# Seven products for gate pairs, the output projection and FFN-out, with the residual kept in DRAM and tables fetched by ACT's queue

## The chip, the cores and the metric

The kernel runs on one core of a Trainium2 chip. The metric is the time of one execution in device microseconds; the median of three runs stands for a kernel. A profile is one further execution with the hardware profiler on, and its times, which are used for all durations here, are in microseconds unless marked ns. TensorE appears as PE (matmuls) and PEld (weight loads), VectorE as DVE, ScalarE as ACT, GpSimd as POOL, SyncE as SP; SPq is SP's queue, from which DMAs are issued.

## The reference

Two layers act on 256 tokens of width 2048, all in float32. A layer is

```python
h = rms_norm(x, g_mix_pre)
proj = h @ w_in                      # 2048 x 11776
u_pool, u_conv, q, k, v, g_ret, gate_pre = split(proj)
y_pool = pool_mixer(u_pool) @ w_pool_proj      # trailing means, 512 -> 2048
y_conv = conv_module(u_conv) @ w_conv_proj     # GLU, causal conv of 31 taps, layer norm, swish
y_ret = retention(q, k, v, g_ret) @ w_ret_proj # 8 heads, rotary, decay, group norm, gate
merged = sigmoid(gate_0) * y_pool + sigmoid(gate_1) * y_conv + sigmoid(gate_2) * y_ret
x = x + rms_norm(merged @ w_out, g_mix_post)
h = rms_norm(x, g_ffn_pre)
a, b = split(h @ w_ffn_in)           # 2048 x 11264
x = x + rms_norm((silu(a) * b) @ w_ffn_out, g_ffn_post)   # 5632 x 2048
```

Nearly all the arithmetic is in the products with `w_in`, `w_ffn_in`, `w_ffn_out` and `w_out`.

## The kernel before

**Products.** The tokens are two halves h of 128. A weight matrix is worked off in chunks of 512 columns; a chunk has kt k-tiles of 128 rows (16 for a width of 2048). One product is one k-tile of one chunk for one half. To keep float32's precision in the faster `fp32r` type, each operand is split into a rounded part and a rest (hi and lo), and a product is three matmuls of 128x128 by 128x512 into one PSUM bank: hi by hi, lo by hi, hi by lo (L747, L748, L749). Activations are split once, by `split` (L127), after a transposition (`transpose4`, L137): four k-tiles of a half in one slot. Weights are split as they come: `load` (L699) takes a block of two k-tiles, fetched by SP's queue into one of six `raw` buffers, casts it on ACT (L725) and subtracts on DVE (L726). There are seven such blocks (`WBLOCKS`), and `load_ahead` keeps them filled.

**Seven products.** Where a chunk n and its partner n + 1 take the same activations, four k-tiles of both, for both halves, form a 2x2 by 2x2 block product, here called a quad: 16 products (2 k-tiles x 2 x 2 x 2 blocks). Seven block products (Winograd's form of Strassen's scheme) do with 14. The kinds are b11, t1, b21, b22, t2, t3 and t4. `load` makes the differences of raw weights they need on DVE (L705, L712, L729, L730), `token_sums` (L174) the sums of activations, and `mixed_product` (L752) puts the results together from PSUM: b11 is copied to a `dt` tile by ACT (L770), t2, t3 and t4 are added to it on DVE (L785 to L797). The banks of b11, t1, t2 and t3 are of the tag `sc`, of which there are four; transpositions and the small matmuls of the jobs use the same four. Plain products accumulate in two `mm` banks for each half. Before the change, only FFN-in's pairs (silu part and linear part) have such a quad, the last one (k-tiles 12 to 15), and the first pair of each layer has none: it is `paired`, its two chunks interleaved plainly.

**Order.** `chunks` (L607 to L640) lists the chunks of a layer: pool stream, v, q, k, swish gate (two each), the conv stream's gate and value, then gates and branch projections, the output, and FFN in four parts of 3, 3, 3 and 2 pairs, each followed by the share of FFN-out that its hidden columns feed, added up in the `og` slots. `items` is the list of k-tiles in order. The main loop (L898) issues half 0's product, and when half 0 is more than `LAG` = 8 items ahead, half 1's; mixed items do both halves at once. Each product counts a tick, and `defer` runs a function so many ticks later (the transposing of results is deferred by 7 or 14).

**Jobs.** Pooling, the convolution, retention and the rotary tables are generators in the list `jobs`. After a product of half 1 of the plain kind, `run_jobs` adds `BUDGET` = 0.35 to a credit (at most 1) and steps the jobs in list order while the credit is above zero; each step yields its cost. A step that yields `WAIT` rests its job for 8 ticks. At most two jobs that aren't `light` are stepped; the convolution is light, with 124 steps of 0.35. Chunks have `needs`: at their first k-tile, `finish` (L325) steps jobs, those not light or named, two at a time in list order, until none named is left, without rests. The code's order is a priority; a scheduler fixes each engine's order from it when the program is built.

**Around it.** `post_collect`, `post_norm` and `pre_norm_quad` (L202 to L240, L161) norm the result of a sub-layer, add it to the residual `xs`, held in SBUF throughout, and make the next activations `xT`. Twenty general buffers of 4 KB a partition (`slot`) hold activations and results; `dt` (two buffers) holds decay and band tables and the sums of the seven products. All DMAs are issued by SP. The beginning (`begin`, L823) is ordered by hand on all engines but GpSimd.

Of the kernel before, what the change touches and what calls it, by code (L numbers as in the profile page):

```python
# [18 lines left out]
P = 128  # L19
# [20 lines left out]
SLOTS = 20  # L40
# [10 lines left out]
N_WARM = 12  # L51

# [23 lines left out]
def trunk(ctx: ExitStack, tc: tile.TileContext, x, x_cols, positions, g_mix_post, g_ffn_post, w_in, pool_w,  # L76
# [38 lines left out]
    xs = []  # L115
    for h in range(2):
        xs.append(cpool.tile([P, 4, NB], F32, name=f"x{h}"))
# [25 lines left out]
    def square_sum(src, acc):  # L143
        j = t2("junk", 1)
        act.activation(j, src, ACT.Square, accum_out=acc)
# [14 lines left out]

    def pre_norm_quad(h, c, gain, mixed):  # L161
        tp, g = transpose4(xs[h][:, c, :]), gain[:, 4 * c:4 * c + 4]
        if not (mixed and c == 3):
            st["xT", h].append(split(tp, g))
            return
        if h == 0:
            st["u"] = slot([P, 2, 4, P])
        u = st["u"][:, h]
        dve.tensor_tensor(u, tp, g.unsqueeze(2).to_broadcast([P, 4, P]), op=ALU.mult)
        st["xT", h].append(split(u))  # L170
        if h == 1:
            defer(6, token_sums)

    def token_sums():  # L174

        u = st["u"]
# [3 lines left out]
        dve.tensor_tensor(s[:, 1], s[:, 0], a11, op=ALU.subtract)  # L180
        dve.tensor_tensor(s[:, 2], a11, a21, op=ALU.subtract)
        dve.tensor_tensor(s[:, 3], a12, s[:, 1], op=ALU.subtract)
        hi, lo = slot([P, 4, 2, P], F32R), slot([P, 4, 2, P], F32R)
        act.copy(hi, s)
        dve.tensor_tensor(lo, s, hi.bitcast(F32), op=ALU.subtract)
        st["S"] = (hi, lo)
# [6 lines left out]
    def sum_squares(h):  # L193
        ssq = small("ssq_n", 4)
        for c in range(4):
            square_sum(xs[h][:, c, :], ssq[:, c:c + 1])
        pre_norm_rstd(h, ssq)

    def load_x(h, c):
        nc.sync.dma_start(xs[h][:, c, :], x[0, h * P:(h + 1) * P, c * NB:(c + 1) * NB])  # L200
# [19 lines left out]
    def post_norm(h, gain, mixed=False):  # L220
# [3 lines left out]
        def residual(c):  # L224
            xc = xs[h][:, c, :]
# [14 lines left out]
        defer(N_FIRST + N_STEP * 4, sum_squares, h)  # L240

# [127 lines left out]
    def pool_job(l, h):  # L369
        if h == 0:  # L370
            pw = slot([P, 4, P])
            nc.sync.dma_start(pw, pool_w[l].rearrange("g c d -> c g d"))
            st["pw"] = pw
        u, pw = st["upool"], st["pw"]
        tabs = []
        for n in ((0,) if h == 0 else (1, 2)):
            b = t2("dt", 2, (P, 4, P))
            nc.sync.dma_start(b, bands[n])
# [16 lines left out]
    def ret_job(l, h, qd):  # L395
# [4 lines left out]
        if h == 0:  # L400
            dt = t2("dt", 2, (P, 4, P))
            nc.sync.dma_start(dt, decays[qd])
# [9 lines left out]
        else:  # L412
            for pr in range(2):
                dt = t2("dt", 2, (P, 4, P))
                nc.sync.dma_start(dt, decays[2 + qd * 2 + pr])
# [97 lines left out]
    def ev_swish(l, qd):  # L513
        def f(h, ps):
# [5 lines left out]
            add_job(("ret", h), ret_job(l, h, qd))  # L520
        return f

    def ev_gate(h, ps):
        s = t2("sg", 3)
        act.activation(s, ps, ACT.Sigmoid, scale=st["rstd", h])  # L525
        st["sg", h] = s

    def ev_y(b, c):
        def f(h, ps):
            if b == 0:  # L530
                if c % 2 == 0:
                    st["mt", h, c // 2] = slot([P, 2, NB])
                dve.tensor_tensor(st["mt", h, c // 2][:, c % 2, :], ps, st["sg", h], op=ALU.mult)
# [3 lines left out]
            dve.tensor_tensor(t, ps, st["sg", h], op=ALU.mult)  # L537
            gp.tensor_tensor(m, m, t, op=ALU.add)  # L538
            if b == 1:
                if c == 0:  # L540
                    st["mT", h] = []
                defer(2 * D_T, lambda: st["mT", h].append(split(transpose4(m))))
        return f

    def gain_tile(c, h, src):
        if h == 0:
            g = t2("gp", 2)
            nc.sync.dma_start(g, src[c * NB:(c + 1) * NB].partition_broadcast(P))
# [9 lines left out]
    def ev_out(l, c):  # L558
        def f(h, ps):
            bc = gain_tile(c, h, g_mix_post[l])  # L560
            og_tile(c, h)
            post_collect(h, c, ps, bc)
            if c == 3:
                post_norm(h, par[l][:, C_GFFN:C_GFFN + 16], True)
        return f

    def ev_a(h, ps):
        t = t2("sg", 3)
        act.activation(t, ps, ACT.Silu, scale=st["rstd", h])  # L569
        st["sg", h] = t  # L570

    def ev_b(first):
        def f(h, ps, mixed=False):
            if first:
                st["hid", h] = []
            t = t2("ta", 3)
            if mixed:
                dve.tensor_tensor(t, st["sum", h], ps, op=ALU.add)  # L578
                ps = t
            dve.scalar_tensor_tensor(t, ps, st["rstd", h], st["sg", h], op0=ALU.mult, op1=ALU.mult)  # L580
            hid = st["hid", h]
            defer(D_T, lambda: hid.append(split(transpose4(t))))
        return f

    def ev_a_sum(h, t, y):

        u = t2("ta", 3)
        dve.tensor_tensor(u, t, y, op=ALU.add)  # L588
        ev_a(h, u)

    def ev_ffn(l, c, part, last):
        def f(h, ps):
            if part == 0:
                act.copy(og_tile(c, h), ps)
                return
            o = st["og", h, c]
            dve.tensor_tensor(o, o, ps, op=ALU.add)  # L597
# [3 lines left out]
            post_collect(h, c, o, bc)  # L601
            if c == 3:
                post_norm(h, par[l + 1][:, C_GPRE:C_GPRE + 16] if l + 1 < DEPTH else None)
# [5 lines left out]

    def add(w, r0, kt, c0, lhs, evac, needs=()):  # L610
        chunks.append((w, r0, kt, c0, lhs, evac, needs))

    for l in range(DEPTH):
        wi = w_in[l]
        add(wi, 0, 16, Q_POOL, "xT", ev_pool(l))
# [8 lines left out]
        add(wi, 0, 16, Q_CG, "xT", ev_conv_g)  # L624
        add(wi, 0, 16, Q_CA, "xT", ev_conv_a(l))
        for b, c in [(b, c) for c in range(4) for b in (0, 2)] + [(1, c) for c in range(4)]:
            add(wi, 0, 16, Q_GATE + b * D + c * NB, "xT", ev_gate)
            w, name = ((w_pool_proj, "pool"), (w_conv_proj, "conv"), (w_ret_proj, "ret"))[b]
            add(w[l], 0, 8 if b == 2 else 4, c * NB, ("brT", b), ev_y(b, c), (name,))
        for c in range(4):  # L630
            add(w_out[l], 0, 16, c * NB, "mT", ev_out(l, c))
        ends.append(len(chunks))
        parts = ((0, 3), (3, 6), (6, 9), (9, 11))
        for p, (b0, b1) in enumerate(parts):
            for j in range(b0, b1):
                add(w_ffn_in[l], 0, 16, j * NB, "xT", ev_a)
                add(w_ffn_in[l], 0, 16, HIDDEN + j * NB, "xT", ev_b(j == b0))
            for c in range(4):
                add(w_ffn_out[l], b0 * 4, (b1 - b0) * 4, c * NB, "hid", ev_ffn(l, c, p, p == len(parts) - 1))
        ends.append(len(chunks))  # L640

    paired = {0} | {e for e in ends[:-1]}
    fast = {n for n, ch in enumerate(chunks) if ch[5] is ev_a and n not in paired}
    items = []
    count = {}

# [4 lines left out]
    while n < len(chunks):  # L653
        if n in fast:
            for k in (0, 2, 4, 6, 8):
                plan("", n, k)
            plan("b11", n, 12)
            plan("t1", n, 12)
            plan("", n, 10)
            plan("b21", n, 14)  # L660
            plan("b22", n, 14)
            plan("", n + 1, 0)
            plan("t2", n, 12)
            plan("", n + 1, 2)
            plan("t3", n, 12)
            plan("", n + 1, 4)
            plan("t4", n, 14)
            for k in (6, 8, 10):
                plan("", n + 1, k)
            n += 2  # L670
        else:
            side = (n, n + 1) if n in paired else (n,)
            for k in range(0, chunks[n][2], LOAD):
                for m in side:
                    plan("", m, k)
            n += len(side)
# [75 lines left out]
    def mixed_product(kind, n, k, w):  # L752

        kk, last = k % 2, k % 2 == 1

        def x_part(h):
            a = st["xT", h][k // 4]
# [204 lines left out]
```

## Time and profile before

| | before |
|---|---|
| median of 3 runs (lowest, highest) | 2876.71 us (2876.64, 2877.05) |
| the profiled execution | 2875.82 us |
| its span | 2874.1 us |
| PE, DVE, ACT busy | 2855.9, 1947.7, 1356.4 us |
| products (three matmuls each) | 4056 |
| granted TensorE clock | 0.999 |
| DMA | 555.07 MB, mean 193 GB/s |

A group's line in the profile names the source line, engine, operation, what it writes and reads (out<-in) and how often, then the busy time and the mean of one in ns, then how long its engine sat idle before it and who ended that. A row of waits names who waited for whom: total us, times, longest us. A row of the windows is the stretch, its length, then busy us of PE, PEld, DVE, ACT and POOL (instructions in brackets), the granted clock, the share of the DMA engines and GB/s. A row of the chain in order of time is start, length, engine, tile and line. PE's busy time counts overlapping matmuls, so the spacing of matmuls, not their length, tells their cost.

### The profile page before, as it was taken

What the parts mean: (1) busy time and instruction counts of PE and PEld (TensorE: products, weight loads), DVE (VectorE), ACT (ScalarE), POOL (GpSimd) and SP (SyncE); (2) the same over time, 40 slices, a digit from 0 to 9 for tenths busy, and PEclk for the clock granted to TensorE, in tenths of its full rate; (3) what the DMA queues carried; (4) which work ended last, traced back from release to release, by engine and by line L of the source; (5) the groups of instructions that cost most, each with busy time, mean ns of one, the idle gap of its engine ahead of it and who ended that gap; (6) DMA issues with size and microseconds to landing.
All of it is one profiled execution on the core that took longest, in us unless ns stands there. A gap on an engine that the chain in (4) does not pass through costs nothing.

```text
span 2874.1 us, 34293 instructions
## 1 busy us (share of the span) xinstructions
PE 2855.9 (99%) x12932; PEld 2362.9 (82%) x12932; DVE 1947.7 (68%) x2253; ACT 1356.4 (47%) x1547; POOL 83.1 (3%) x102
## 2 busy tenths in 40 slices
PE   9999999999999999999999999999999999999998
PEld 7788888888888888888888888888888888888887
DVE  6766965555775776857765569555567757668586
ACT  5444445444644544544554444444455454445353
POOL 0000000000000000000000000001000000000000
PEclk9999999999999999999999999999999999999999
DMA  8655565556565656555655555655565555666554
GB/s 298 193 183 176 186 199 189 191 189 203 174 204 174 215 196 201 176 203 175 229 188 185 189 171 188 199 189 186 191 204 190 190 185 189 211 194 200 187 183 153
DMA packets 289862, 555.07 MB, mean 193 GB/s; under 512 B 17824, under 2 KB 21152, under 8 KB 289696
## 3 DMA queue, kind: packets, MB, share of 16 engines
q1 hardware_dynamic: 289696, 552.89, 58.5%
q8 instruction: 101, 1.65, 0.2%
q14 instruction: 65, 0.53, 0.1%
HBM read 550.72 MB, written 2.10 MB: 192 GB/s over the span
## 4 chain that ended last, share of the span: by engine, by line
PE 98%; DVE 1%; DMA 0%; POOL 0%; ACT 0%; issue 0%; SPq 0%; DVEq 0%; POOLq 0%; ACTq 0%
PE mm L748 32%; PE mm L749 32%; PE mm L747 32%; PE tp L140 2%; DVE x L226 0%; PE sc L429 0%; PE tp L421 0%; PE sc L385 0%; DVE wlo L726 0%; DVE ta L131 0%; DMA dt<-in_bands 0%; DMA par<-in_params 0%; POOL rpost_a L210 0%; PE sc L411 0%; PE tp L406 0%
## 5 line engine op out<-in xcount | busy, mean ns | idle before, releaser
L726 DVE TENSOR_TENSOR wlo<-raw,whi 128x1024 fp32r<-128x1024 f32 (+1 forms) x1085 | 1336.9, 1240 | 738.0 <-ACT whi L725 725.6
L725 ACT CAST whi<-raw 128x1024 fp32r<-128x1024 f32 (+1 forms) x1085 | 1135.4, 1052 | 1283.5 <-PE mm L748 1148.2
L747 PE MATMUL mm<-whi,slot 128*128 128x512 f32 x4056 | 1589.9, 392 | 1.9 <-ACT whi L725 1.7
L748 PE MATMUL mm<-whi,slot 128*128 128x512 f32 x4056 | 1581.1, 390 | 0.2
L749 PE MATMUL mm<-wlo,slot 128*128 128x512 f32 x4056 | 1580.9, 390 | 0.0
L749 PEld LDWEIGHTS mm<-wlo,slot 128*128 128x128 f32 x4056 | 761.8, 188 | 159.4 <-DVE wlo L726 0.7
L747 PEld LDWEIGHTS mm<-whi,slot 128*128 128x128 f32 x4056 | 762.0, 188 | 156.7 <-ACT whi L725 2.4
L748 PEld LDWEIGHTS mm<-whi,slot 128*128 128x128 f32 x4056 | 762.4, 188 | 156.1 <-DVE slot L134 2.1
L342 DVE SCALAR_TENSOR_TENSOR slot<-slot,par,slot 128x229 f32<-128x229 f32 (+23 forms) x240 | 101.9, 479 | 0.3
L134 DVE TENSOR_TENSOR slot<-tp,slot 128x512 fp32r<-128x512 f32 x60 | 41.2, 687 | 50.3 <-ACT slot L133 50.3
L133 ACT CAST slot<-tp 128x512 fp32r<-128x512 f32 x60 | 35.2, 586 | 83.3 <-PE tp L140 83.3
L538 POOL TENSOR_TENSOR slot<-slot,tb 128x512 f32<-128x512 f32 x32 | 43.3, 1352 | 639.5 <-DVE tb L537 639.5
L578 DVE TENSOR_TENSOR ta<-dt,mm 128x512 f32<-128x512 f32 x40 | 27.4, 684 | 29.9 <-PE mm L749 29.9
L218 POOL TENSOR_SCALAR ms_o<-ssq_t 128x1 f32<-128x1 f32 x8 | 3.2, 395 | 1509.0 <-DVE ssq_t L216 1509.0
L525 ACT ACTIVATE sg<-mm,rstd 128x512 f32<-128x512 f32 x48 | 33.0, 688 | 24.4 <-PE mm L749 24.2
L597 DVE TENSOR_TENSOR slot<-slot,mm 128x512 f32<-128x512 f32 x48 | 32.8, 684 | 13.0 <-PE mm L749 13.0
L140 PEld LDWEIGHTS tp<-ident,ta 128*128 128x128 f32 x272 | 34.0, 141 | 8.4
L140 PE MATMUL tp<-ident,ta 128*128 128x128 f32 x272 | 40.6, 271 | 0.0
L569 ACT ACTIVATE sg<-ta,rstd 128x512 f32<-128x512 f32 x40 | 29.0, 725 | 10.5 <-DVE ta L588 10.5
L580 DVE SCALAR_TENSOR_TENSOR ta<-ta,rstd,sg 128x512 f32<-128x512 f32 x40 | 30.0, 749 | 1.0
L133 ACT CAST slot<-ta 128x512 fp32r<-128x512 f32 x36 | 22.4, 621 | 16.4 <-DVE ta L131 16.2
L537 DVE TENSOR_TENSOR tb<-mm,sg 128x512 f32<-128x512 f32 x32 | 22.1, 690 | 9.4 <-PE mm L749 8.1
(131 smaller groups left out, 732.5 us busy)
## 6 DMA issues: line engine op xcount, KB each, us to landing
raw<-in_w_in SPq DMA_DIRECT2D x367, 512.0 KB, 3.5
raw<-in_w_ffn_in SPq DMA_DIRECT2D x352, 512.0 KB, 4.4
raw<-in_w_ffn_out SPq DMA_DIRECT2D x176, 512.0 KB, 3.7
raw<-in_w_out SPq DMA_DIRECT2D x64, 512.0 KB, 3.6
raw<-in_w_ret_proj SPq DMA_DIRECT2D x32, 512.0 KB, 3.6
raw<-in_w_pool_proj SPq DMA_DIRECT2D x16, 512.0 KB, 3.6
raw<-in_w_conv_proj SPq DMA_DIRECT2D x16, 512.0 KB, 3.8
dt<-in_decays SPq DMA_DIRECT2D x12, 256.0 KB, 3.8
```

The costliest lines, as they stand in the source:

```text
L133: act.copy(t[:, 0], src)
L134: dve.tensor_tensor(t[:, 1], src, t[:, 0].bitcast(F32), op=ALU.subtract)
L140: pe.transpose(tp[:, j, :], src[:, j * P:(j + 1) * P], ident)
L342: dve.scalar_tensor_tensor(acc[:, ct, s:], hT[:, ct, :SEQ - s], w[:, TAPS - 1 - s:TAPS - s], acc[:, ct, s:], op0=ALU.mult, op1=ALU.add)
L525: act.activation(s, ps, ACT.Sigmoid, scale=st["rstd", h])
L538: gp.tensor_tensor(m, m, t, op=ALU.add)
L597: dve.tensor_tensor(o, o, ps, op=ALU.add)
L725: act.copy(hi[:, kk:kk + step], raw[:, kk:kk + step])
L726: dve.tensor_tensor(lo[:, kk:kk + step], raw[:, kk:kk + step], hi[:, kk:kk + step].bitcast(F32), op=ALU.subtract)
L747: pe.matmul(ps, a[0], w[0], start=first, stop=False)
L748: pe.matmul(ps, a[1], w[0], start=False, stop=False)
L749: pe.matmul(ps, a[0], w[1], start=False, stop=stop)
```

## The change

More products are done by seven instead of eight block products, and what that needs is rearranged:

- A pair of chunks names its mixed quads with `mix(...)`. The gates of pool and conv for the same columns become one pair (quad 3), the retention gates for two neighbouring column chunks another (quads 2 and 3). The four output chunks are two pairs (quad 0, the first quad made), and so are the four FFN-out chunks of each part. FFN-in stays as it was.
- `token_sums` becomes a light job for one quad of given activations; it rebuilds them by adding hi and lo. Chunks need "sum" (or "sum2").
- The order of a layer is pool, conv gate, conv value, then v, q, k, swish for each quad of heads; gates and projections are grouped by pairs; FFN has three parts of 4, 4 and 3 pairs.
- The evictions take a tile t of sums to be added to their bank.
- The residual lives in DRAM: `fetch_x` loads it into slots in the middle of a sub-layer's last chunks, `store_x` stores it 28 ticks after `post_norm`. Slots rise from 20 to 24; `junk` goes, `sg` has four buffers.
- The tables of pooling and decay, the pooling weights, the gains and x are fetched by ACT's DMA queue instead of SP's.

```diff
-SLOTS = 20
+SLOTS = 24
+N_STORE = 28
...
+    def fetch_x(n, h):
+        st["x", h] = []
+        for c2 in range(2):
+            t = slot([P, 2, NB])
+            nc.scalar.dma_start(t, xd[n][h][:, columns(c2)].rearrange("p (c n) -> p c n", n=NB))
+            st["x", h].append(t)
+    def store_x(n, h, tiles):
+        for c2 in range(2):
+            nc.sync.dma_start(xd[n][h][:, columns(c2)].rearrange("p (c n) -> p c n", n=NB), tiles[c2])
...
+    def token_sums(lhs, c):
+        ts = [st[lhs, h][c] for h in range(2)]
+        u = slot([P, 2, 4, P])
+        for h in range(2):
+            dve.tensor_tensor(u[:, h], ts[h][:, 0].bitcast(F32), ts[h][:, 1].bitcast(F32), op=ALU.add)
+            yield 0.7
...
+        st["S", lhs, c] = (hi, lo)
+        yield 1.2
...
-            nc.sync.dma_start(dt, decays[qd])
+            nc.scalar.dma_start(dt, decays[qd])
...
             add_job(("ret", h), ret_job(l, h, qd))
+            if qd == 1 and h == 1:
+                add_job(("sum", 0), token_sums("xT", 3), True)
+                add_job(("sum2", 0), token_sums("xT", 2), True)
...
-            nc.sync.dma_start(g, src[c * NB:(c + 1) * NB].partition_broadcast(P))
+            nc.scalar.dma_start(g, src[c * NB:(c + 1) * NB].partition_broadcast(P))
...
+            if t is not None:
+                u = t2("ta", 3)
+                dve.tensor_tensor(u, t, ps, op=ALU.add)
+                ps = u
             post_collect(h, c, ps, bc)
+            if c == 1:
+                fetch_x(2 * l, h)
...
+                if t is not None:
+                    dve.tensor_tensor(o, o, t, op=ALU.add)
+                dve.tensor_tensor(o, o, ps, op=ALU.add)
...
         add(wi, 0, 16, Q_POOL, "xT", ev_pool(l))
+        add(wi, 0, 16, Q_CG, "xT", ev_conv_g)
+        add(wi, 0, 16, Q_CA, "xT", ev_conv_a(l))
         for qd in range(2):
             add(wi, 0, 16, Q_V + qd * NB, "xT", ev_v(qd))
-        for qd in range(2):
             add(wi, 0, 16, Q_Q + qd * NB, "xT", ev_rot("qT", qd))
-        for qd in range(2):
             add(wi, 0, 16, Q_K + qd * NB, "xT", ev_rot("kT", qd))
-        for qd in range(2):
             add(wi, 0, 16, Q_R + qd * NB, "xT", ev_swish(l, qd))
...
         for c in range(4):
+            mix(3)
+            for b in range(2):
+                gate(b, c, ("sum",))
+            for b in range(2):
+                project(b, c)
+        for c2 in range(2):
+            mix(2, 3)
+            for c in range(2):
+                gate(2, 2 * c2 + c, ("sum2",))
+            for c in range(2):
+                project(2, 2 * c2 + c)
+        for c in range(4):
+            if c % 2 == 0:
+                mix(0)
+            add(w_out[l], 0, 16, c * NB, "mT", ev_out(l, c), ("sum",))
...
-        parts = ((0, 3), (3, 6), (6, 9), (9, 11))
+        parts = ((0, 4), (4, 8), (8, 11))
...
             for c in range(4):
+                if c % 2 == 0:
+                    mix(0)
+                add(w_ffn_out[l], b0 * 4, (b1 - b0) * 4, c * NB, "hid", ev_ffn(l, c, p, last), ("sum",))
...
+    SEVEN = (("b11", 0), ("t1", 0), ("b21", 2), ("b22", 2), ("t2", 0), ("t3", 0), ("t4", 2))
...
+        if n in mixed:
+            ks = [k for k in ks if k // 4 not in mixed[n]]
+            head = max(LAG // LOAD, len(ks) - 1) if len(mixed[n]) == 1 else len(ks)
+            for k in ks[:head]:
                 plan("", n, k)
+            for q in mixed[n][:-1]:
+                for kind, d in SEVEN:
+                    plan(kind, n, 4 * q + d)
+            q = 4 * mixed[n][-1]
+            plan("b11", n, q)
+            plan("t1", n, q)
+            for k in ks[head:]:
+                plan("", n, k)
+            plan("b21", n, q + 2)
+            plan("b22", n, q + 2)
+            for k, kind, kq in zip(ks, ("t2", "t3", "t4"), (q, q, q + 2)):
                 plan("", n + 1, k)
+                plan(kind, n, kq)
+            for k in ks[3:]:
+                plan("", n + 1, k)
```

More of the change, by code (lines that the diff above doesn't have):

```diff
@@ L377, in pool_job @@
             b = t2("dt", 2, (P, 4, P))
[L378 removed]
+            nc.scalar.dma_start(b, bands[n])
             tabs.append(b)
@@ L520, in f, with ev_gate @@
             add_job(("ret", h), ret_job(l, h, qd))
-        return f
[L523 to L526, printed above, removed]
+            if qd == 1 and h == 1:
+                add_job(("sum", 0), token_sums("xT", 3), True)
+                add_job(("sum2", 0), token_sums("xT", 2), True)
+        return f
+    def ev_gate(b, c):
+        def f(h, ps, t=None):
+            s = t2("sg", 4)
+            if t is not None:
+                dve.tensor_tensor(s, t, ps, op=ALU.add)
+                ps = s
+            act.activation(s, ps, ACT.Sigmoid, scale=st["rstd", h])
+            st["sg", h, b, c] = s
+        return f
     def ev_y(b, c):
         def f(h, ps):
+            g = st["sg", h, b, c]
             if b == 0:
@@ L565, in ev_out, with ev_a, f @@
         return f
[L567 to L570, printed above, removed]
+    def ev_a(h, ps, t=None):
+        if t is not None:
+            u = t2("ta", 3)
+            dve.tensor_tensor(u, t, ps, op=ALU.add)
+            ps = u
+        s = t2("sg", 4)
+        act.activation(s, ps, ACT.Silu, scale=st["rstd", h])
+        st["sg", h] = s
     def ev_b(first):
-        def f(h, ps, mixed=False):
+        def f(h, ps, t=None):
@@ L574, in f @@
             if first:
                 st["hid", h] = []
[L576 to L580, printed above, removed]
-            hid = st["hid", h]
-            defer(D_T, lambda: hid.append(split(transpose4(t))))
-        return f
[L585 to L589, printed above, removed]
+            u = t2("ta", 3)
@@ L591, in ev_ffn, with put, f @@
+            if t is not None:
+                dve.tensor_tensor(u, t, ps, op=ALU.add)
+                ps = u
+            dve.scalar_tensor_tensor(u, ps, st["rstd", h], st["sg", h], op0=ALU.mult, op1=ALU.mult)
+            hid = st["hid", h]
+            def put():
+                hid.append(split(transpose4(u)))
+                if first and h == 1:
+                    add_job(("sum", 0), token_sums("hid", 0), True)
+            defer(D_T, put)
+        return f
     def ev_ffn(l, c, part, last):
-        def f(h, ps):
-            if part == 0:
+        def f(h, ps, t=None):
+            if part == 0 and t is None:
@@ L608, in trunk, with mix, gate, project @@
     ends = []
+    mixed = {}
     def add(w, r0, kt, c0, lhs, evac, needs=()):
         chunks.append((w, r0, kt, c0, lhs, evac, needs))
+    def mix(*quads):
+        mixed[len(chunks)] = quads
     for l in range(DEPTH):
         wi = w_in[l]
+        def gate(b, c, needs=()):
+            add(wi, 0, 16, Q_GATE + b * D + c * NB, "xT", ev_gate(b, c), needs)
+        def project(b, c):
+            w, name = ((w_pool_proj, "pool"), (w_conv_proj, "conv"), (w_ret_proj, "ret"))[b]
+            add(w[l], 0, 8 if b == 2 else 4, c * NB, ("brT", b), ev_y(b, c), (name,))
@@ L778, in mixed_product @@
             product((0, n + 1), "mm0", s_part(3), w, False)
-        elif kind == "t4":
-            y = product((1, n), "mm1", x_part(1), w, last)
-            if last:
-                assert items[done[1]][1:] > (n, 11)
-                s = st["sum", 1]
-                ev_a_sum(1, s, y)
-                dve.tensor_tensor(s, s, banks["t1", n], op=ALU.add)
         elif kind == "t2":
@@ L795, in mixed_product @@
             if last:
-                s = st["sum", 1]
+                s = st["sum", 1, n]
                 dve.tensor_tensor(s, s, x, op=ALU.add)
+        elif kind == "t4":
+            y = product((1, n), "mm1", a_part(1), w, last)
+            if last:
+                assert items[done[1]][1:] > (n, final[n])
+                s = st["sum", 1, n]
+                outs[0](1, y, s)
+                dve.tensor_tensor(s, s, banks["t1", n], op=ALU.add)
     def multiply(h):
```

158 lines of the change are left out of this document (75 added, 83 removed).

## The prediction

> **What bounds the kernel now.** I read the page's head, the engine shares and the chain first, then who TensorE waited for, then the groups by line.
>
> ```profile
> span 2874.1 us, 34293 instructions
> PE 2855.9 (99%) x12932; PEld 2362.9 (82%) x12932; DVE 1947.7 (68%) x2253; ACT 1356.4 (47%) x1547; POOL 83.1 (3%) x102
> PE 98%; DVE 1%; DMA 0%; POOL 0%; ACT 0%; issue 0%; SPq 0%; DVEq 0%; POOLq 0%; ACTq 0%
> ```
> ```profile
> PE sc L385 <- DMA dt<-in_bands: 3.0, 1, 3.0
> PE mm L747 <- ACT whi L725: 1.7, 1, 1.7
> PE tp L140 <- DVE x L226: 1.6, 4, 0.6
> PE sc L858 <- DVE slot L826: 1.5, 1, 1.5
> PE mm L747 <- ACT slot L133: 0.2, 1, 0.2
> ```
> ```profile
> L747 PE MATMUL mm<-whi,slot 128*128 128x512 f32 x4056 | 1589.9, 392 | 1.9 <-ACT whi L725 1.7
> ```
>
> The reader is to see that 98% of the chain is TensorE and that all its waits add up to 8 us. So time is the number of matmuls times their spacing. L747 runs once per product (three matmuls), so there are 4056 products. Their spacing comes from one seven-product pair of FFN-in. In the chain in order of time its transposes stand at
>
> ```profile
> 773.98 0.44 PE tp L140 x4
> 806.43 0.44 PE tp L140 x4
> 817.10 0.44 PE tp L140 x4
> ```
>
> One period is 817.10 - 773.98 = 43.12 us for 62 products and two groups of transposes: (43.12 - 0.88) / 62 = **0.681 us a product**. VectorE in that stretch, by line:
>
> ```profile
> L726 DVE TENSOR_TENSOR wlo<-raw,whi 128x1024 fp32r<-128x1024 f32 x19 | 22.9, 1220 | 4.4 <-ACT whi L725 4.3
> L580 DVE SCALAR_TENSOR_TENSOR ta<-ta,rstd,sg 128x512 f32<-128x512 f32 x2 | 1.5, 748 | 0.0
> L134 DVE TENSOR_TENSOR slot<-tp,slot 128x512 fp32r<-128x512 f32 x2 | 1.4, 691 | 2.7 <-ACT slot L133 2.7
> L578 DVE TENSOR_TENSOR ta<-dt,mm 128x512 f32<-128x512 f32 x2 | 1.4, 682 | 1.3 <-PE mm L749 1.3
> L705 DVE TENSOR_TENSOR raw<-raw,raw 128x1024 f32<-128x1024 f32 x1 | 1.2, 1225 | 0.0
> L790 DVE TENSOR_TENSOR dt<-dt,mm 128x512 f32<-128x512 f32 x1 | 0.7, 689 | 0.3 <-PE mm L749 0.3
> ```
>
> ```profile
> 774.00:817.00 43.00, 43.00 (x195) 35.59 (x194) 34.24 (x35) 22.48 (x24) 0.00 (x0) 1.00 0.59 196
> L725 ACT CAST whi<-raw 128x1024 fp32r<-128x1024 f32 x19 | 19.8, 1052 | 16.2 <-PE mm L748 10.4 <-DVE raw L705 2.6 <-issue 1.8
> ```
>
> These are 19 weight loads, four raw differences (L705 and three like it), four bank sums (L790 and three like it) and the evictions. The row of the windows gives VectorE (third number) 34.24 of 43 us, 80% busy (the lines add up to 36, since their ends overlap), and TensorE does not wait.
>
> **What the change takes away.** A quad (four k-tiles, two chunks, two halves of tokens) costs 16 products, or 14 as seven. Before, ten quads a layer are mixed (FFN-in but its first pair). After, I count a layer: 4 (gate pairs of pool and conv) + 4 (two retention pairs, two quads each) + 2 (output) + 10 (FFN-in) + 6 (three parts of FFN-out, two pairs each) = 26. That is 32 quads more over two layers, 64 products less, 3992 in all: 64 x 0.681 = **43.6 us**. No transpose or small matmul is added or removed.
>
> **What it adds.** On VectorE, for 32 quads: 3 loads and 4 differences each, 7 x 1.22 = 8.5 us; for 28 more pairs, four bank sums and four adds at eviction, 8 x 0.68 = 5.5 us; twelve more `token_sums` at two adds of 0.68, four small ones near 0.4 (estimated as half of 0.68 and a fixed part) and one of 1.22, 4.2 us; less 16 accumulations of 0.68, for FFN-out has three parts instead of four. 272 + 154 + 50 - 11 = 465 us, so VectorE goes from 1948 to about 2413, 85% of the new span. ACT gains some 130 us (96 casts of 1.05, copies), far from full. Mean shares decide nothing; the stretches do:
>
> - Gate pairs of pool and conv, output pairs, FFN-out parts 0 and 1 have the 19 loads of the quoted stretch and not more evictions: at most its share, no stall. I cost them at nothing; the seven weight blocks loaded ahead hide them, and without these each quad would expose 4 differences, 4.9 us. Output now begins at quad 1, so merged quad 3 is wanted four products (2.7 us) after its transposes are issued; 0.44, a cast and a split near 0.7 each (L134's row) fit, and a late one costs 1 at most.
> - Retention gates: 60 products, 40.9 us, need 22 loads, 8 differences, 8 adds: 36.6 + 5.4 = 42.0 us, 103%. The two projections behind them (32 products, 21.8 us, 8 loads and 8 small ones, 15.3 us) pay it back.
> - FFN-out's last part: 46 products a pair, 31.3 us; 15 loads, 4 differences, 4 bank sums and 12 adds and products: 23.2 + 10.9 = 34.1 us, 109%. Two pairs overrun by 5.5 us; seven blocks ahead are 7 x 1.22 = 8.5 us of work done. Between 0 and 5.5 a layer I take 1.
>
> **The retention jobs** are where I looked longest. Reordered, `conv_job` joins the list after the third chunk, ahead of every `ret_job`. Each half-1 product earns 0.35 of credit, a conv step costs 0.35, and it has 124: it eats the credit of 7.75 chunks. Only eight lie between its start and the first gate, so the four `ret_job`s of a layer stand almost untouched when `finish` for "sum" is called at half 1 of the first gate, and `finish` steps jobs in list order: all four are issued there in one go, without their pauses. Their VectorE part, from the stretch 190 to 283 that holds them before:
>
> ```profile
> L441 DVE TENSOR_SCALAR ta<-sc,gnmv,gnr 128x128 f32<-128x128 f32 x16 | 5.8, 405 | 5.4 <-POOL gnr L124 5.4
> L434 DVE BATCH_NORM_STATS2 gnst<-sc 128x6 f32<-128x128 f32 x16 | 3.6, 281 | 0.2 <-PE sc L429 0.2
> L424 DVE TENSOR_TENSOR ta<-tp,dt 128x512 f32<-128x512 f32 x4 | 2.8, 688 | 0.4 <-PE tp L421 0.2
> L444 DVE TENSOR_TENSOR tb<-ta,slot 128x512 f32<-128x512 f32 x4 | 2.7, 681 | 0.0
> L436 DVE BATCH_NORM_AGGREGATE gnmv<-gnst 128x2 f32<-128x6 f32 x16 | 1.4, 149 | 0.0
> L408 DVE TENSOR_TENSOR ta<-tp,dt 128x512 f32<-128x512 f32 x2 | 1.4, 683 | 0.0
> ```
>
> with the scaling and splitting (8 x 0.69) 23 us; a group of their matmuls is one of these:
>
> ```profile
> 196.09 0.89 PE tp L406 x8
> 202.43 0.89 PE sc L411 x8
> ```
>  What hides it: the order of an engine's instructions isn't that of the code. Conv's adds are issued by credit over some 290 products, about 200 us, yet VectorE was through with them long before their transposes:
>
> ```profile
> L342 DVE SCALAR_TENSOR_TENSOR slot<-slot,par,slot x21: 443/451/458, 359.7 to 375.0; 128x232 f32<-128x232 f32 x2, 128x231 f32<-128x231 f32 x2, 128x230 f32<-128x230 f32 x2, 128x229 f32<-128x229 f32 x2
> L349 PE MATMUL tp<-ident,slot x16: 270/272/273, 459.9 to 1905.2; 128*128 128x128 f32 x16
> ```
> ```profile
> 280.00:380.00 100.00, 100.00 (x447) 82.88 (x446) 97.82 (x173) 43.57 (x46) 3.57 (x2) 1.00 0.58 189
> ```
>
> So ready work is drawn ahead, and with VectorE at 98% for 100 us (third number) TensorE stayed full. Behind the flush TensorE has matmuls that need neither a retention result nor one of the four `sc` banks: 10 of half 1, four at k = 10 and 11, b21, b22 and t4 (6), 24 of the partner chunk: 44 products, 30 us. VectorE owes 23 + 4 (sums) + some 23 (16 loads, 3 differences) = 50 against 30 + 12 us of small matmuls + 8.5 of lead: level. A wait on a table, as the 3.0 us for the bands, can come on top. Bounds 0 and 40 a layer (rival 3); the nearest rows are the full stretch and the 3.0, so I take 2.5.
>
> **Queues.** 52 issues go to ACT (36 tables and gains, 16 of x). The largest wait that moves along, and the price of one such issue's data:
>
> ```profile
> SPq L548 <- DVE slot L213: 20.8, 11, 10.5
> dt<-in_decays SPq DMA_DIRECT2D x12, 256.0 KB, 3.8
> ```
>
> On SP raw fetches stood behind it; on ACT the casts will, and TensorE behind them. Seven blocks are 9.5 us of mixed products or 19 of plain ones: 10.5 is covered, bounds 0 to 1 each; I take 0. Three stores and four fetches of x (2 MB each) are 14 MB beside some 550, on engines 58% busy (DMA share in the row above), nothing. Between stages, columns 2 and 3 now end one behind the other and gain an add: 0.7 at three borders and in the tail, which lasts until
>
> ```profile
> 2858.40 0.70 DVE slot L597
> 2869.18 1.33 DVE x L226 x2
> ```
>
> **The sum.** Stalls: 2 x 2.5 + 2 x 1 + 4 x 0.7 = 9.8, less chances that the 3.0 us of the bands go: I say 8.5. The profiled execution took 2875.8 (span 2874.1 and 1.7 around it), 0.9 under the median 2876.7. 2875.8 - 43.6 + 8.5 = 2840.7, on the median's scale **2841.6**.
>
> **Rivals.**
>
> 1. The flush is half covered: the table waits recur for the four late decay tables, 3 to 4 us each, and VectorE, in order, stands: 12 to 16 a layer. 2833 + 25 = 2858. For: two `dt` buffers for six tables and then the bank sums. Against: TensorE never waited for decays before.
> 2. VectorE's full stretches are paid at face value: 4 x 1.1 + 4 x 2.8 = 15.6 us, and the flush's 5: 2853. For: the sums above; four `sc` banks stay taken over both retention quads. Against: the 98% stretch. [...]
> 3. Slower: the flush stands bare at the head of the first gate of each layer. Two rounds of two jobs, each as long as two tables of 3.8, four groups of matmuls of 0.9, decay products 1.4, statistics 1.7, the 1.4 for POOL (idle in L441's row over four), scaling 2.3, transposing and splitting 2.4: some 20, a layer 40, both 80: 2833 + 80 = 2913. It decides from 21.8 us a layer, that is if less than 18 of the 40 are covered. For: nothing in the code parts the jobs. Against: work is drawn ahead, see above.
> 4. The products fall and the time doesn't, because TensorE isn't the bound: the 43.6 us turn into waiting, 2876. For: its weight loads are busy only 82%. Against: it waited 8 us in all, and the spacing of 0.681 holds with VectorE at 80% and at 98%. That fewer than 64 products go I can't see; it is arithmetic. [...]
>
> **Chances.** Forecast (2831 to 2850) 0.66; rival 1 0.14; rival 2 0.09; rival 3 0.07; rival 4, and whatever else ends near no change, 0.04. The range goes from 2830 (no stall, bands' wait gone) to 2866. A run can tell 0.2%, 5.8 us: faster 0.89, same 0.04, slower 0.07.
>
> **What would show it.** L747's line x3992; spacing 0.681 unchanged; TensorE's waits under 20 us, the largest at the first gates (by the rows below less the jobs that now come later, and half of the saving for the second: near 270 and 1680 us); retention's transposes bunched there; VectorE near 2400 busy. A list of waits for `dt`, or of idle TensorE beside VectorE at 100% in the first gates, would put rival 1 or 3 in its place; gaps in FFN-out's last part rival 2.
>
> ```profile
> 283.65 0.87 PE tp L140 x8
> 1712.71 0.87 PE tp L140 x8
> ```

## The result, and the profile after

The changed kernel takes 2902.69 us (median of four runs, 2900.93 to 2905.39) against 2876.68 before (2875.59 to 2877.05): **26 us slower**, a ratio of 1.0092 with a 95% interval of 1.0074 to 1.0109. I had forecast 2841.6, 35 us faster. The sign was wrong, and the time lies far above the range (2830 to 2866).

The head of the page after, its chain and the line of the first matmul of a product:

```profile
span 2903.6 us, 34791 instructions
PE 2836.6 (98%) x12740; PEld 2335.6 (80%) x12740; DVE 2345.4 (81%) x2773; ACT 1460.4 (50%) x1668; POOL 111.9 (4%) x102
PE 89%; DVE 6%; DMA 2%; issue 1%; POOL 1%; ACT 1%; SPq 0%; DVEq 0%; POOLq 0%; ACTq 0%
L830 PE MATMUL mm<-whi,slot 128*128 128x512 f32 x3992 | 1567.1, 393 | 9.7 <-ACT whi L808 5.0
```

The 64 products are gone (x3992), and TensorE's share of the chain fell from 98% to 89%. Who TensorE waited for, and the clock granted to it over the whole span, after and before:

```profile
PE tp L142 <- DVE tb L461: 17.6, 6, 5.0
PE mm L832 <- DVE wlo L809: 10.3, 11, 2.3
PE tp L142 <- DVE slot L242: 6.2, 7, 2.8
PE mm L830 <- ACT whi L808: 5.0, 4, 3.7
PE mm L830 <- ACT slot L135: 4.5, 3, 4.0
PE tp L142 <- DVE ta L373: 3.5, 3, 2.7
```
```profile
core 0: 2903.6 us, clock 0.991
```
```profile
core 0: 2874.1 us, clock 0.999
```

The page's PE idle time went from 2874.1 - 2855.9 = 18.2 to 2903.6 - 2836.6 = 67.0 us, 49 us more. The clock took another part: (1 - 0.991) of 2903.6 is 26 us, (1 - 0.999) of 2874.1 is 3. Together some 72 us were lost where 43.6 were saved; the spans differ by 29.5, so the two accounts agree within about 1 us, which is as near as a clock rounded to 0.001 allows. (The profiled execution, 2905.4, is the slowest of the four.)

Where the loss sits is read from the windows after (length; busy us of PE, PEld, DVE, ACT and POOL; granted clock; DMA share; GB/s):

```profile
255.00:300.00 45.00, 41.15 (x219) 34.02 (x217) 33.14 (x63) 16.59 (x19) 5.39 (x6) 1.00 0.42 132
300.00:360.00 60.00, 47.74 (x207) 38.56 (x208) 47.05 (x73) 28.30 (x42) 4.70 (x7) 0.89 0.44 146
1740.00:1800.00 60.00, 49.41 (x232) 40.47 (x231) 51.34 (x86) 28.75 (x44) 7.25 (x9) 0.91 0.48 158
1400.00:1480.00 80.00, 71.29 (x310) 57.69 (x310) 72.91 (x98) 42.41 (x68) 8.65 (x10) 0.94 0.70 245
```

Two stretches lie at the first gates of the two layers. From 255 to 360 TensorE idled 3.9 + 12.3 us and lost 0.11 x 60 = 6.6 to the clock: 22.7 together. In the second layer 1740 to 1800 gives 10.6 + 5.4 = 16.0. The fourth is the border from the first layer's FFN to the second layer: 8.7 + 4.8 = 13.5, where the kernel before idled 27.0 - 25.1 = 1.9 at full clock (the row below). VectorE is not at 98% in the gate stretches (47 and 51 of 60 us) but is near full at the border (72.9 of 80).

```profile
1426.00:1453.00 27.00, 25.08 (x119) 18.96 (x118) 23.82 (x35) 16.53 (x32) 5.53 (x7) 1.00 0.55 176
```

### The profile page after: what moved, and what is told of

Its sections match the earlier page's. It is cut to its first block, busy times and chain, and to the rows that moved or that the text cites. A ratio compares the mean times of both kernels' runs of the same rounds, so it can differ in the third digit from the quotient of the medians.

```text
span 2903.6 us, 34791 instructions
## 1 busy us (share of the span) xinstructions
PE 2836.6 (98%) x12740; PEld 2335.6 (80%) x12740; DVE 2345.4 (81%) x2773; ACT 1460.4 (50%) x1668; POOL 111.9 (4%) x102
## 4 chain that ended last, share of the span: by engine, by line
PE 89%; DVE 6%; DMA 2%; issue 1%; POOL 1%; ACT 1%; SPq 0%; DVEq 0%; POOLq 0%; ACTq 0%
PE mm L832 29%; PE mm L831 29%; PE mm L830 29%; DVE wlo L809 2%; PE tp L142 2%; DMA raw<-in_w_ffn_out 1%; ACT whi L808 1%; DVE slot L242 0%; DVE ta L458 0%; DVE slot L136 0%; POOL gnr L126 0%; DMA raw<-in_w_ret_proj 0%; DMA raw<-in_w_in 0%; DVE raw L788 0%; DVE ta L133 0%
## 5 line engine op out<-in xcount | busy, mean ns | idle before, releaser
L808 ACT CAST whi<-raw 128x1024 fp32r<-128x1024 f32 (+1 forms) x1181 | 1223.2, 1052 | 1174.5 <-PE mm L831 773.5
L809 DVE TENSOR_TENSOR wlo<-raw,whi 128x1024 fp32r<-128x1024 f32 (+1 forms) x1181 | 1433.3, 1233 | 367.3 <-ACT whi L808 354.3
L830 PE MATMUL mm<-whi,slot 128*128 128x512 f32 x3992 | 1567.1, 393 | 9.7 <-ACT whi L808 5.0
L832 PE MATMUL mm<-wlo,slot 128*128 128x512 f32 x3992 | 1559.1, 391 | 10.3 <-DVE wlo L809 10.3
L831 PE MATMUL mm<-whi,slot 128*128 128x512 f32 x3992 | 1559.7, 391 | 0.8 <-DVE slot L136 0.3
L832 PEld LDWEIGHTS mm<-wlo,slot 128*128 128x128 f32 x3992 | 751.7, 188 | 172.8 <-DVE wlo L809 15.7
L830 PEld LDWEIGHTS mm<-whi,slot 128*128 128x128 f32 x3992 | 751.9, 188 | 167.4 <-ACT whi L808 8.9
L831 PEld LDWEIGHTS mm<-whi,slot 128*128 128x128 f32 x3992 | 752.7, 189 | 156.7 <-DVE slot L136 3.0
L359 DVE SCALAR_TENSOR_TENSOR slot<-slot,par,slot 128x229 f32<-128x229 f32 (+25 forms) x240 | 98.4, 466 | 0.5
L135 ACT CAST slot<-tp 128x512 fp32r<-128x512 f32 x60 | 35.2, 586 | 86.7 <-PE tp L142 86.7
L564 POOL TENSOR_TENSOR slot<-slot,tb 128x512 f32<-128x512 f32 x32 | 56.1, 1757 | 572.5 <-DVE tb L563 572.5
L788 DVE TENSOR_TENSOR raw<-raw,raw 128x1024 f32<-128x1024 f32 x52 | 63.6, 1224 | 1.7
L813 DVE TENSOR_TENSOR raw<-raw,raw 128x1024 f32<-128x1024 f32 x52 | 63.5, 1221 | 1.0
L812 DVE TENSOR_TENSOR raw<-raw,raw 128x1024 f32<-128x1024 f32 x52 | 63.4, 1219 | 0.5
L795 DVE TENSOR_TENSOR raw<-raw,raw 128x1024 f32<-128x1024 f32 x52 | 63.3, 1217 | 0.2
L135 ACT CAST slot<-ta 128x512 fp32r<-128x512 f32 x40 | 24.5, 619 | 67.5 <-DVE ta L133 61.6
L142 PE MATMUL tp<-ident,ta 128*128 128x128 f32 x272 | 40.8, 272 | 3.5 <-DVE ta L373 3.5
L142 PEld LDWEIGHTS tp<-ident,ta 128*128 128x128 f32 x272 | 33.8, 141 | 12.8 <-DVE ta L373 4.1
L549 ACT ACTIVATE sg<-sg,rstd 128x512 f32<-128x512 f32 x48 | 34.3, 723 | 11.4 <-DVE sg L547 11.3
```

Of the source, the lines that this page charges most:

```text
L135: act.copy(t[:, 0], src)
L142: pe.transpose(tp[:, j, :], src[:, j * P:(j + 1) * P], ident)
L359: dve.scalar_tensor_tensor(acc[:, ct, s:], hT[:, ct, :SEQ - s], w[:, TAPS - 1 - s:TAPS - s], acc[:, ct, s:], op0=ALU.mult, op1=ALU.add)
L788: dve.tensor_tensor(kept["b11"], kept["b12"], kept["b11"], op=ALU.subtract)
L795: dve.tensor_tensor(kept["b21"], kept["b21"], kept["b22"], op=ALU.subtract)
L808: act.copy(hi[:, kk:kk + step], raw[:, kk:kk + step])
```

## The experiments

Each of them is the changed kernel with the edit shown. Theory A is that the bunched retention jobs starve TensorE, B that VectorE simply has too much to do there, C that ACT's DMA queue delays tables and casts.

**Only the named jobs are stepped by `finish`.**

```diff
-            for job in [job for job in jobs if not job[3] or job[0] in keys][:2]:
+            for job in [job for job in jobs if job[0] in keys][:2]:
```

> finish steps only the jobs that are named, so that the call for the sums at the first gate issues the sums alone and the four retention jobs come later, by credit. Theory A (the bunched retention jobs cost some 42 us of TensorE time, 24 in the first layer and 18 in the second): about 2866 us, TensorE's waits for L461 gone, the granted clock near 0.998. Theory B (VectorE has too much to do around the first gates, and the same work only moves): 2890 us or more, the waits turn up a few gates later. Theory C (ACT's DMA queue): no change, 2903.

Measured: 2869.64 us, ratio to the kernel before 0.9973 (0.9962 to 0.9984), 33 us less than the changed kernel. One line turned the loss into a small gain. The same stretches of the windows, and its two largest waits:

```profile
300.00:360.00 60.00, 56.30 (x278) 47.08 (x278) 48.17 (x76) 31.07 (x44) 7.20 (x10) 0.97 0.47 148
1740.00:1800.00 60.00, 60.00 (x291) 49.88 (x290) 52.50 (x75) 30.48 (x35) 8.50 (x6) 1.00 0.57 182
```
```profile
PE tp L142 <- DVE slot L242: 6.4, 7, 3.0
PE mm L832 <- DVE wlo L809: 5.2, 6, 1.8
```

VectorE is as busy as in the changed kernel (48.2 and 52.5 of 60 us), but TensorE issues 278 instead of 207 matmuls in the first stretch. So A, not B: at the gates it was not the amount of VectorE work that cost, but what was issued when. L461, the retention result that TensorE waited 17.6 us for, is gone from the waits, as A asked; the time is 3.6 above A's number, which took all of the 42 us for recoverable, and the clock is 0.995, not A's 0.998: the border and the end still lose theirs (below). The edit changes two things at once, for the sums come early and the bunch is gone; the last experiment takes them apart.

**The retention jobs ahead of the convolution.**

```diff
-            add_job(("ret", h), ret_job(l, h, qd))
+            at = next((i for i, job in enumerate(jobs) if job[0][0] == "conv"), len(jobs))
+            jobs.insert(at, [("ret", h), ret_job(l, h, qd), 0, False])
```

> The retention jobs stand ahead of the convolution in the list; finish is as in the changed kernel. Theory A: the first three retention jobs of a layer are through before the first gate, the fourth is still bunched with the sums, and the convolution's end may be late for its projection: some 30 us of the 42 come back, 2870 to 2876. Theory B: 2890 or more. Theory C: 2903.

Measured: 2881.76 us (1.0018, 1.0009 to 1.0028), 21 us less than the changed kernel, where A expected some 30. It confirms that it was the convolution that held the jobs back, but mending it this way is the weaker cure: the fourth job still comes in one go with the sums, and TensorE now waits for weight splits,

```profile
PE mm L833 <- DVE wlo L810: 16.6, 12, 3.6
```

6 us more of them than after (10.3). That these come from the convolution's adds, which now are later and meet the flush, is argued, not shown. Its waits for the retention result L461 are gone.

**Tables by SP's queue again** (`nc.scalar.dma_start` back to `nc.sync.dma_start` for pooling weights, bands, decays and gains).

> Tables, pooling weights and gains are fetched by SP's queue again (x stays with ACT's). Theory A and B: within 4 us of the changed kernel, 2899 to 2907. Theory C (a table behind casts on ACT's queue is late, and casts behind it): 2885 or less.

Measured: 2900.01 us (1.0080, 1.0065 to 1.0095), 2.7 less than the changed kernel, and the runs of the two just touch (2898.26 to 2901.67, 2900.93 to 2905.39). C is out as the cause; what little there is sits at the very start (below).

**The last part of FFN-out plain.**

```diff
-                if c % 2 == 0:
+                if c % 2 == 0 and not last:
                     mix(0)
```

> FFN-out's last part of each layer is done with plain products again: 8 products more, 5.4 us of TensorE. If VectorE's overrun in that part is what costs 3.8 us there, 9.8 more at the border to the second layer and 4.2 near the end: 2889 to 2895. If the border's loss comes from the residual in DRAM and the late columns: 2904 to 2908.

Measured: 2889.78 us (1.0044, 1.0029 to 1.0059), 12.9 less although eight products, 5.4 us, were added. So these four mixed pairs cost 18 us in stalls to save 5.4. The border, over the same 80 us as above, in this kernel:

```profile
1400.00:1480.00 80.00, 78.03 (x356) 63.16 (x355) 57.45 (x75) 41.78 (x66) 7.30 (x10) 1.00 0.69 228
```

TensorE idles 2.0 us instead of 8.7 and keeps its clock, VectorE has air (57 of 80), and x still comes from DRAM. The residual in DRAM alone is therefore not what the border paid for. How the part falls behind is seen in the timelines of ACT and VectorE in the changed kernel, between 1408 and 1420 us:

```profile
1410.17 1.05 ACT L808 CAST whi<-raw 128x1024 fp32r<-128x1024 f32 x1 [5.18 <-DMA raw<-in_w_ffn_out]
```
```profile
1411.26 1.22 DVE L809 TENSOR_TENSOR wlo<-raw,whi 128x1024 fp32r<-128x1024 f32 x1 [3.08 <-ACT whi L808]
```

Casts wait for raw weights, and VectorE for a cast: it is idle here, not overrun. SP's queue had waited for the raw differences before it could fetch (1340 to 1425 us):

```profile
SPq L775 <- DVE raw L813: 27.9, 3, 13.5
```

So the six raw buffers, four of which a quad holds while its differences are made, have their part: late differences make late fetches, late fetches late casts, and the lead of seven blocks isn't there when it is needed. VectorE's work is then crowded into the border, where it is busy 29.9 of the 30 us from 1420 to 1450. Whether the buffers or VectorE's load came first, no run tells apart.

**Both edits**: `finish` and the plain last part.

> Both edits: finish steps the named jobs alone, and FFN-out's last part is plain. If the two losses are separate, they add up: 2902.7 - 33.1 - 12.9 = 2856.7. If the retention bunch and the crowded border only share one lack of VectorE, less: 2862 or more.

Measured: 2856.60 us (0.9932, 0.9915 to 0.9948), 0.1 from the sum of the two. They are separate losses. The granted clock is back at 0.998.

**A budget of 0.5** on top of both (`BUDGET = 0.5`).

> As e5_named_and_plain_last, with a budget of 0.5 for the jobs instead of 0.35, so that the convolution's layer norm is issued before its projection asks for it (6.2 us lost between 306 and 369 us of e1_finish_named). If it is lateness of issue that costs there: 4 to 7 us less than e5. If VectorE is full there and the work only competes earlier: no change or up to 5 more.

Measured: 2853.93 us (0.9923, 0.9908 to 0.9938), 2.7 less than e5, short of the 4 to 7 expected; the runs of the two kernels touch (2855.39 to 2857.72, 2852.47 to 2855.55). The wait for the convolution's norm, which is 3.2 us in e1 and e5 (L142 <- DVE ta L373), is no longer among the longest waits, and TensorE's idle time from 300 to 360 us falls from 3.7 (e5) to 0.1. So it was lateness of issue, as far as these runs can tell 2.7 us from none.

**One quad in the retention gates** on top of both (`mix(3)`, and no sums for quad 2).

> As e5_named_and_plain_last, with one quad instead of two in the retention gates: 8 products more, 5.4 us of TensorE. The retention gates lose about 5 us in two places (2.5 and 2.4 in e1_finish_named). If VectorE's 103% over two quads in a row causes that: the same as e5 within 2 us, and no loss there. If the banks or something else causes it: 4 to 6 us more than e5.

Measured: 2860.83 us (0.9945, 0.9930 to 0.9960), 4.2 more than e5: of the 5.4 us that the eight products cost, only 1.2 comes back. That is the second of the two expectations: the 103% of VectorE does not cause the losses near the retention gates, and what does was not looked into. Two quads in a row pay.

**The output's second pair plain** on top of both (`if c == 0: mix(0)`).

> As e5_named_and_plain_last, with the output's second pair plain: 4 products more, 2.7 us. The border to FFN loses 3.7 us in each layer against 0.9 before. If that comes from columns 2 and 3 ending one behind the other: 3 us less than e5. If it comes from x in slots and DRAM: 3 us more.

Measured: 2854.69 us (0.9925, 0.9910 to 0.9940), 1.9 less than e5 where four products, 2.7 us, were added: that pair costs 4.6 us of stalls in two layers. The wait of the border's transposes for the residual, before and after this edit (e5, then this kernel):

```profile
PE tp L142 <- DVE slot L242: 4.1, 7, 0.8
```
```profile
PE tp L142 <- DVE slot L242: 0.7, 1, 0.7
```

So the column that ends right behind its neighbour, not x from DRAM, is late at that border too.

**Both of these, and then the tables too.**

> e6_budget and e8_out_one_pair together (named jobs alone in finish, last part of FFN-out plain, budget 0.5, the output's second pair plain). If the losses are separate: 2856.6 - 2.7 - 1.9 = 2852.0. If the convolution's lateness and the border share VectorE: 2854 or more.

> As e9_budget_and_out, with tables, pooling weights and gains on SP's queue. The start loses 9.7 us with ACT's queue and 6.1 with SP's (e3_tables_sp), since ACT issues two tables and two gains in the first 3 us, beside the first weights: 2.5 to 3.5 us less than e9, 2849. If that difference was chance: within 1 of e9.

Measured: e9 2854.44 us (2851.1 to 2855.51; 0.9927, 0.9913 to 0.9940). The median lies on the side of "share VectorE", but the runs lie on both, and the profiled execution (2853.25) holds something else:

```profile
563.85 10.33 POOL L564 TENSOR_TENSOR slot<-slot,tb 128x512 f32<-128x512 f32 x1 [10.58 <-DVE tb L563]
```
```profile
PE tp L142 <- POOL slot L564: 4.1, 1, 4.1
```

GpSimd's add of a merged column took 10.3 us once; on average it takes 1.35 in the kernel before and 1.76 in the changed kernel. TensorE waited 4.1 us for it, and lost 5.9 us to idle time and clock from 540 to 600, against 1.2 in e10. Why it was slow, and whether it was so in the other four runs, is not known; so e9 does not settle its question. e10: **2849.59 us** (2846.7 to 2852.18; 0.9911, 0.9897 to 0.9924), 4.9 less than e9 and the fastest kernel of this study, 25 us faster than before. The windows show the start of e9 and of e10:

```profile
0.00:15.00 15.00, 10.61 (x27) 5.45 (x28) 5.22 (x9) 4.70 (x8) 0.68 (x6) 0.89 0.90 301
```
```profile
0.00:15.00 15.00, 12.21 (x38) 6.16 (x38) 7.16 (x13) 6.73 (x10) 0.68 (x6) 1.00 0.89 300
```

With the tables on ACT's queue TensorE has issued 27 matmuls by 15 us, with SP's 38. In its first 60 us e9 loses 6.6 us to idle time and clock, e10 3.4. That difference is the 2.5 to 3.5 us that was expected. The two profiled executions lie 6.6 apart, and the slow add accounts for the rest. In the timeline of the changed kernel ACT asks for two band tables and two gains before 3 us:

```profile
0.72 0.89 ACTq L395 DMA_DIRECT2D dt<-in_bands  x2
1.64 0.97 ACTq L580 DMA_DIRECT2D gp<-in_g_mix_post  x2
```

1 MB that is wanted later goes beside the first weights while the DMA engines are 90% busy.

**The sums first, then all four retention jobs at once.** The engines' order of the changed kernel, TensorE's instructions with buffer numbers, shows what stood behind the bunch (not a profile, but the built program):

```
L142 MATMUL tp_475_2487<-ident_73,tb_474_2484 128x128 x4
L830 MATMUL mm_485_2524<-whi_413_2256,slot_69_381 128x512
...
L830 MATMUL mm_490_2547<-whi_417_2280,slot_479_2502 128x512
L830 MATMUL mm_505_2621<-whi_492_2563,slot_479_2502 128x512
L830 MATMUL mm_506_2634<-whi_498_2606,slot_479_2502 128x512
L830 MATMUL mm_516_2675<-whi_503_2617,slot_479_2502 128x512
```

tp_475 is the last retention job's transposition. Behind it come b11 (mm_485), and then t1, b22, t2 and t3. These four read slot_479: the sums of activations, which `finish` had issued last. (b11 reads no sums; like t1, t2 and t3 it writes one of the four `sc` banks.) So the experiment issues them first and leaves the bunch as it is:

```diff
+        named = any(job[0] == ("sum", 0) for job in jobs) and ("sum", 0) in keys
         while any(job[0] in keys for job in jobs):
-            for job in [job for job in jobs if not job[3] or job[0] in keys][:2]:
+            for job in [job for job in jobs if job[0] in keys][:2]:
+                step_job(job)
+        while named and any(job[0][0] == "ret" for job in jobs):
+            for job in [job for job in jobs if not job[3]][:2]:
```

> The changed kernel, but the call at the first gate issues the sums of activations before the four retention jobs, which it still issues all at once. In TensorE's order of the changed kernel, b22, t1, t2 and t3 of the first gate pair and half 0 of the partner chunk stand behind the last retention transposes, since they need the sums. If that is what starves TensorE (the seven weight blocks fill with products that wait for sums): most of the 42 us come back, 2865 to 2875. If the bunch itself costs (its chain of latencies, four banks): little comes back, 2893 or more.

Measured: 2886.62 us (2883.31 to 2894.99; 1.0047, 1.0030 to 1.0064), 16 less than the changed kernel and 17 more than e1: between the two, so both count. Its windows at the gates of both layers, three of its waits (over the whole run), and its products between the bunch's first matmul and its last transposition (270.2 to 312.5 us; L836 is the last matmul of a product):

```profile
255.00:300.00 45.00, 44.05 (x233) 36.65 (x231) 37.19 (x72) 18.50 (x20) 5.38 (x6) 1.00 0.43 130
300.00:360.00 60.00, 51.66 (x237) 41.49 (x237) 52.31 (x72) 32.10 (x46) 8.62 (x8) 0.94 0.48 149
1740.00:1800.00 60.00, 56.02 (x254) 44.60 (x255) 56.68 (x76) 36.53 (x51) 7.52 (x8) 1.00 0.57 181
```
```profile
PE mm L836 <- DVE wlo L813: 9.3, 8, 2.0
PE mm L834 <- ACT slot L135: 8.8, 4, 4.8
PE tp L142 <- DVE tb L465: 1.8, 4, 0.6
```
```profile
L836 PE MATMUL mm<-wlo,slot 128*128 128x512 f32 x34 | 13.3, 400 | 2.1 <-DVE wlo L813 2.0
```

In the stretches shown the changed kernel loses 22.7 and 16.0 us to idle time and clock, this one 12.9 and 4.0, e1 5.5 and none. By the profiles, then, some 22 us come from the sums and 11 from the bunch; the medians say 16 and 17, with runs of e11 that lie 12 us apart. What the bunch still costs is not its own chain: TensorE's waits for retention results (L461, here L465) fell from 17.6 us to 1.8. At the two gates it waits for weight splits instead, 4.3 us, and once, for 4.8 us, for the convolution's activations (L135, at 337 us). In this kernel's built program b22 and the partner's first products stand ahead of the last retention transposition; b11, t1, t2 and t3 still stand behind it.

## Why the prediction was wrong

**What held.** The products (3992) and the kind of the saving: with most of the stalls mended the time falls by 25 us with 4004 products, of the 35 that 52 products less are worth. The reading that the convolution eats the jobs' credit and that all four retention jobs come out of one `finish` (e1, e2). VectorE's load in the gate pairs and in FFN-out's first two parts: TensorE is never idle from 360 to 540 and from 780 to 1380 us.

**The step that failed** is this one: "Behind the flush TensorE has matmuls that need neither a retention result nor one of the four `sc` banks: 10 of half 1, four at k = 10 and 11, b21, b22 and t4 (6), 24 of the partner chunk: 44 products, 30 us." From 271.5 to 312.8 us, from the first small matmul to the last transposition of the bunch, TensorE did 21 products (the line of that stretch; L830 is the first matmul of a product):

```profile
L830 PE MATMUL mm<-whi,slot 128*128 128x512 f32 x21 | 8.5, 404 | 0.0
```

By the program's order 20 of them are of those 44, and one was left over from half 0. I had asked of each product whether it needs a retention result or a bank, and not whether it needs the sums. b22 does (two products), and the partner's half 0 (twelve) adds to b22's bank, so these stood behind the bunch as well. The other ten lacked their weights, for a product that can't run holds its weight block. ACT's timeline of the changed kernel shows the lead running out:

```profile
291.33 2.95 ACT L808 CAST whi<-raw 128x1024 fp32r<-128x1024 f32 x3 [4.31 <-DVE raw L813]
294.18 0.61 ACT L135 CAST slot<-ta 128x512 fp32r<-128x512 f32 x1
303.67 0.62 ACT L135 CAST slot<-ta 128x512 fp32r<-128x512 f32 x1 [8.88 <-DVE ta L133]
314.65 0.62 ACT L135 CAST slot<-ta 128x512 fp32r<-128x512 f32 x1 [10.36 <-DVE ta L133]
316.01 1.05 ACT L808 CAST whi<-raw 128x1024 fp32r<-128x1024 f32 x1 [0.74 <-PE mm L831]
316.96 1.04 ACT L202 CAST slot<-slot 128x1024 fp32r<-128x1024 f32 x1
317.91 0.58 ACT L855 COPY dt<-mm 128x512 f32<-128x512 f32 x1
```

No weight is cast between 294.3 and 316.0. By the program's order the seven blocks held b11, t1, b22, t2, t3 and two of the partner's; the sums were cast at 316.96, and b11, planned as the fourth product after the bunch began, was copied at 317.91. "Seven blocks ahead" is a lead only while the blocks turn over. With the sums issued first (e11), TensorE does 34 products in that stretch, and half to two thirds of the loss is gone; the rest goes when the bunch goes (e1). My price for the flush, "I take 2.5" a layer, compares with 22.7 and 16.0; the break-even of rival 3, 21.8 a layer, was nearly reached by this alone. Rival 3 had the place and the bunch that stands bare, in part; it did not have the sums and the held blocks either. That the measured time comes near its 2913 is luck in part, since 18 us of the loss are FFN-out's.

**FFN-out's last part.** The sum gave 109% of VectorE, and the time that I drew from it was wrong: "Between 0 and 5.5 a layer I take 1." It cost about 9 a layer (18 in all, e4), more than the whole overrun. The sum adds up the lengths of single instructions, whose ends overlap (36 against 34.24 us in the prediction's own stretch), so by busy time it is nearer 104%. I had put the seven blocks against the overrun as if they were full when the part began and as if nothing followed. I had not counted the raw buffers that a quad holds, and the part ends in the border, where the norm's chain needs VectorE at once. How the 9 us divide among these was not tried apart.

**Terms mis-sized.** VectorE's growth: 465 us forecast, 398 measured (1947.7 to 2345.4). ACT's queue: "I take 0", measured 2.7 (e3) and some 3 of e10's 4.9, not through casts behind a waiting table, which I looked for, but through what is fetched first at the start. Columns 2 and 3 ending one behind the other: 0.7 at a border, measured 2.3 for the output's (e8). Retention's two quads: forecast at 103% without a stall, and right to keep (e7). Conv's late norm, not priced: 2.7 (e6).

**The term that was missing** is the clock. I priced waits and not what follows them. By the method above 23 of the 72 us lost are clock. Windows of the changed kernel, cut to the stretches around the end of the bunch:

```profile
298.60:302.00 3.40, 0.76 (x5) 0.32 (x4) 2.75 (x7) 0.00 (x0) 0.62 (x1) 1.00 0.47 154
302.00:305.40 3.40, 3.40 (x17) 3.40 (x18) 3.37 (x4) 0.62 (x1) 0.00 (x0) 0.52 0.38 114
305.50:308.90 3.40, 1.67 (x12) 1.29 (x11) 2.80 (x9) 0.00 (x0) 0.00 (x0) 0.99 0.59 183
309.00:315.80 6.80, 3.00 (x9) 2.56 (x10) 4.07 (x12) 0.62 (x1) 1.20 (x2) 0.50 0.00 0
316.00:349.80 33.80, 29.43 (x135) 23.47 (x135) 27.52 (x35) 22.43 (x31) 2.17 (x4) 1.00 0.56 187
```

and the matmuls in the fourth of them, from TensorE's timeline:

```profile
314.11 0.63 PE L831 MATMUL mm<-whi,slot 128*128 128x512 f32 x1
314.54 0.63 PE L832 MATMUL mm<-wlo,slot 128*128 128x512 f32 x1
314.96 0.63 PE L830 MATMUL mm<-whi,slot 128*128 128x512 f32 x1
```

They start 0.43 us apart, where a third of 0.681, 0.227, is usual; from 316 us on the clock is whole again. Behind the wait of 2.6 us (until 301.96) the granted clock was 0.52 for 3.4 us, and from the middle of the one of 4.9 us (until 312.80) it was 0.50 for 6.8. Ahead of these stretches (the first and the third row) it was 1.00 and 0.99, with 0.76 and 1.67 us of matmuls there. With most of these waits gone (e5) it is 0.998 over the whole span.

**What stays open.** e9 doesn't settle whether the budget and the output's pair add up. How what stays of the bunch in e11 divides between weight splits, the convolution, the four banks and the clock was not tried apart.

## What to carry to other kernels

When a stall is said to be covered by ready work, list for each covering instruction all that it reads and the accumulation that it continues, and ask whether the buffers of the work that can't run are the ones that feed the work that can: a prefetch of seven blocks stops when seven blocked products hold them (here from 294.3 to 316.0 us). A call that must have one small job done should do that job, not everything ahead of it in the list. And ask what follows a wait as well as how long it is: here a wait of 2.6 us on TensorE was followed by 3.4 us at a clock of 0.52.

## What the runs showed of the hardware

Two things I had not expected. TensorE's granted clock went to half right after a wait of 2.6 us in the changed kernel (0.52 from 302.0 us) and in the middle of one of 4.9 (0.50 from about 309), but not after the 3.0 us wait for the bands in the kernel before (until 78.7 us; 1.00 from 75 to 83), nor after the 2.7 us wait for the same bands in the changed kernel (until 81.6 us; 1.00 from 78 to 86). So the length of one gap didn't decide alone; what else did, no run here tells apart. And with the tables on ACT's queue four of them, 256 KB each, were issued before 2.7 us (the changed kernel's timeline), and TensorE issued 27 matmuls in its first 15 us (e9), against 38 with the tables on SP's queue (e10).

How much faster `fp32r` is than float32 shows in the kernel before. The bands' matmuls (L385) are plain float32 of 128x128, each with two rows in the trace (24 for the first layer's twelve). Seven of them, from 78.68 us to the next matmul at 80.26, took 0.226 us each, as long as one `fp32r` matmul with four times the columns (128x512, 0.227).
